# Splitting weight tiles with two DMAs instead of ScalarE and VectorE

## The chip, the cores and the metric

The kernel runs on one core of a Trainium2 chip. The metric is the device time of one execution in microseconds (us). Before the change it is 1057.51 us, the median of three runs (1057.33 to 1058.59). In what follows PE is TensorE, ACT is ScalarE, DVE is VectorE, POOL is GpSimd and SP is SyncE, whose queue issues all DMAs of the kernel before. PEld is TensorE's loading of weights, which runs beside its matmuls.

## The reference

One layer of a decoder trunk on a sequence of 512 tokens and 1024 channels, in float32. After a root-mean-square norm, one matrix `w_in` (1024 x 10 128) projects the tokens into queries, keys and values for three groups of dilated window attention, into the input of a causal pooling branch, into the inputs of a state-space branch (SSD), and into three gates. Each branch ends in its own matrix (`w_a`, `w_b`, `w_c`), the gated sum goes through `w_o` and is added to the input. Then come a second norm, a feed-forward part with a short causal convolution (`ffn_w_up`, 1024 x 5632, and `ffn_w_down`, 2816 x 1024), the second residual and a last norm:

```python
u = rmsnorm(x, ln1_g[i])
proj = u @ w_in[i]
...
merged = gates[:, :, 0] * y_a + gates[:, :, 1] * y_b + gates[:, :, 2] * y_c
x = x + merged @ w_o[i]
x = x + conv_ffn(rmsnorm(x, ln2_g[i]), ffn_w_up[i], ffn_conv_w[i], ffn_conv_b[i], ffn_w_down[i])
return rmsnorm(x, final_g)
```

## The kernel before

**Three products for one.** Every large product is computed in TensorE's type fp32r, which keeps fewer bits than float32. To keep the precision, both operands are split into a high part (the value rounded to fp32r) and a low part (the value less its high part, rounded again), and `mm3` (L215) adds three products in PSUM: high x high, high x low of the activation, and low of the weight x high. The low part of a weight tile is thus first read in the last third of the first block of a job's products.

**Jobs.** All weights are cut into 94 tiles. One tile is a `Job` (L72): its sources in DRAM, its shape and a `body` that issues the products. Most tiles hold 1 MB, as 8 blocks of 128 rows by 256 columns (`jobs_a`, L230: two chunks of 24 matmuls of 512 columns) or as 4 blocks by 512 columns (`jobs_b`, L243: four blocks of tokens, 12 matmuls each). The 8 tiles of `w_o` also hold 1 MB, but each serves two of the four blocks of tokens only, so that its job has 24 matmuls. The tiles of the values are 0.75 or 0.78 MB, the two of `w_a` 0.75 MB, and the last of each half of `w_down` 0.5 MB. The order of the jobs is that of `program` (L1098): pooling input (4 jobs), gate 1 (4), the pooling matrix (1), `w_b` (4); for each attention group values (2) and queries with keys (3), with the SSD inputs (6) after the second group; gate 0 (4), the SSD gate z (4) and gate 2 (4) mixed, `w_a` (2), `w_c` (4), `w_o` (8), `ffn_w_up` (22), `ffn_w_down` (12).

**How a tile comes in.** There are three steps, each with a pool of buffers:

- `fetch` (L168): SP issues the load from DRAM into `raw` (2 buffers).
- `cast` (L177): ACT copies `raw` into `wh` (3 buffers), type fp32r, in two halves.
- `lows` (L197): DVE writes `raw` less `wh` into `wl` (2 buffers), in one instruction.

The main loop (L1273 to L1299) issues, ahead of the products of job n, `prepare` (L1281): the low part of tile n + 1, the cast of tile n + 2 and the load of tile n + 3. With two `raw` buffers the load of tile n + 3 has to wait until the low part of tile n + 1 has been computed. The cast's halves are not issued at once: they are put into the list `second`, and every call of `step` (L143, after each chunk of products) issues one of them; what is left is issued at the start of the next job (L1278). The first four tiles are prepared by hand (L1227 to L1270).

**Order of work.** The instructions of PE, ACT, DVE and POOL run in the order in which the program writes them (`ORDERED`, L1304); each engine is a queue, and an instruction that waits holds up those behind it. `step` also moves along the generators of side work: attention items (`attend`, L489), SSD items (`ssd_item`, L759), norms. POOL's own work is small: the running sums of the pooling branch (`pool_evac`, L621), scalings of the SSD (L787, L802), sums of squares (L865), the attention's weighting (L604), the sum of the branches (L914), half of a norm (L330) and the product of the feed-forward part (L1008). SP's queue holds the weight loads and, among them, the small loads of the side work: `vr` (L468), `al` and `ea` (L766, L772), `wb` (L602).

PSUM has two groups of four banks (`bufs=4`, L101): "mm" for the chunks of the jobs and "sm" for the side work. A chunk's result must be read by ACT or DVE before its bank is used again four chunks later.

Of the kernel before, what the change touches and what calls it, by code (L numbers as in the profile page):

```python
# [10 lines left out]
F32 = mybir.dt.float32  # L11
F32R = mybir.dt.float32r
AF = mybir.ActivationFunctionType
OP = mybir.AluOpType
AX = mybir.AxisListType

P = 128
# [64 lines left out]
def trunk(ctx: ExitStack, tc, out, x, rel_bias, ln1_g, w_in, b_gate, w_a, pool_w, pool_scale, w_b,  # L82
# [3 lines left out]
    act, dve, pool, pe, sp = nc.scalar, nc.vector, nc.gpsimd, nc.tensor, nc.sync  # L86
# [6 lines left out]
    rows = ctx.enter_context(tc.tile_pool(name="rows", bufs=1))  # L93
    wraw = ctx.enter_context(tc.tile_pool(name="wraw", bufs=2))
    whp = ctx.enter_context(tc.tile_pool(name="whp", bufs=3))
    wlp = ctx.enter_context(tc.tile_pool(name="wlp", bufs=2))
    upool = ctx.enter_context(tc.tile_pool(name="upool", bufs=1))
    big = ctx.enter_context(tc.tile_pool(name="big", bufs=NBIG))
    ypool = ctx.enter_context(tc.tile_pool(name="ypool", bufs=2))
# [35 lines left out]
    second = []  # L135

    def flush():
        todo = second[:]
        second.clear()
        for f in todo:  # L140
            f()
# [26 lines left out]
    def fetch(job, cuts=1):  # L168
        raw = job.raw = wraw.tile([P, job.k, job.c], F32, name="raw", tag="raw")
        at = 0  # L170
        for src in job.parts:
            n = src.shape[-1] // cuts
            for i in range(cuts):
                sp.dma_start(raw[:, :, at:at + n], src[:, :, i * n:(i + 1) * n])
                at += n

    def cast(job, cuts=1, spread=False):  # L177

        w = job.c // cuts
        job.high = whp.tile([P, job.k, job.c], F32R, name="wh", tag="wh")  # L180

        def high(i):
            o = slice(i * w, (i + 1) * w)
            act.copy(job.high[:, :, o], job.raw[:, :, o])  # L184

        def at(i):
            high(i)
            if i + 1 < cuts:
                second.append(lambda: at(i + 1))

        if spread:
            second.append(lambda: at(0))
            return
        for i in range(cuts):
            high(i)

    def lows(job, cuts=1, eng=None):  # L197

        w, h = job.c // cuts, job.high
        l = wlp.tile([P, job.k, job.c], F32R, name="wl", tag="wl")  # L200
        job.split = h, l
        for i in range(cuts):
            o = slice(i * w, (i + 1) * w)
            (eng or dve).tensor_tensor(l[:, :, o], job.raw[:, :, o], h[:, :, o].bitcast(F32),  # L204
                                       OP.subtract)
            yield

    def low(job, cuts=1, eng=None):
        for _ in lows(job, cuts, eng):
            pass  # L210
# [926 lines left out]
    weights = [j for j in jobs if isinstance(j, Job)]  # L1137
# [87 lines left out]
    pe.transpose(first[2][:, :KD], g8[:KD, :P], eye[:KD, :KD])  # L1225
    dve.tensor_copy(g1, first[2][:, :KD])
    cast(weights[0], 2)  # L1227
    low(weights[0], 2, pool)
    for k in range(KD):
        turn_scale(1, k % 2 * 4 + k // 2)  # L1230
    for k in range(KD):
        turned(k, 0, bank(k))
    cast(weights[1], 2)
    parts = lows(weights[1], 2)

# [28 lines left out]
    fetch(weights[3])  # L1264
    begin(0, 256, S)
    cast(weights[2])
    low(weights[2])
    begin(1, 256, S)
# [4 lines left out]
    n = 0  # L1273
    for job in jobs:
        if not isinstance(job, Job):
            job.fn()
            continue
        while second:  # L1278
            flush()
        if n >= 2:  # L1280
            def prepare(n=n, later=False):  # L1281

                def rest():
                    if n + 1 < len(weights):
                        low(weights[n + 1])
                    if n + 2 < len(weights):
                        cast(weights[n + 2], 2, spread=not later)
                    if n + 3 < len(weights):
                        fetch(weights[n + 3])
                if later:  # L1290
                    return rest
                rest()

            if job.late:
                job.prepare = prepare
            else:
                prepare()
            job.body(job.split)
        n += 1  # L1299
# [2 lines left out]

# [1 line left out]
ORDERED = {EngineType.PE, EngineType.Activation, EngineType.DVE, EngineType.Pool}  # L1304
NBIG = 54
MIX = "ZZ0zz1ggggaa"
SSD_ORDER = ((0, 0, 1), (1, 0, 1), (0, 1, 1), (2, 0, 1), (1, 1, 1), (3, 0, 1), (2, 1, 1), (3, 1, 1))
WARM = 12
# [29 lines left out]
```

## Time and profile before

| What | Value |
|---|---|
| Median of three runs | 1057.51 us (1057.33 to 1058.59) |
| The profiled execution's own time | 1058.24 us |
| Its span in the trace | 1056.4 us |
| PE busy | 1044.1 us, 99% |
| DVE busy | 576.7 us, 55%; of it 219.2 us in 94 computations of low parts (L204) |
| ACT busy | 430.9 us, 41%; of it 187.2 us in 186 casts of high parts (L184) |
| POOL busy | 134.9 us, 13%, and no DMA is issued from it |
| DMA queue of the loads and stores | 114.68 MB, 35.9% of 16 engines' span |
| Mean TensorE clock granted | 0.998 |

The page has six parts: busy time of each engine; the span in 40 slices; the DMA queues; the chain of work that ended last, followed back through what released each step; the costliest groups of instructions, with busy time, mean length and the idle time of the engine just before them; and the DMA issues. Further views, used below, are the list of waits (who waited for whom), the timeline (instructions in order of time, equal ones merged) and the table of windows (for chosen stretches: busy time of each engine, granted clock, share of the 16 DMA engines in use, GB/s). A matmul's end in the trace is modelled, so "busy" on PE does not mean that it works at its peak; the distance from one matmul's start to the next tells more. The 24 matmuls of one chunk take 5.44 us, so a job of 48 takes 10.9 us and a job of `w_o` about 5.7 us with what lies between.

### The profile page before, as it was taken

To read this page: it belongs to the slowest core of one execution; us is meant where nothing else is said; L and a number is where in the kernel's file an instruction comes from. 1 tells how busy PE (TensorE), PEld (TensorE's weight loads), DVE (VectorE), ACT (ScalarE), POOL (GpSimd) and SP (SyncE) were. 2 spreads that over 40 slices of the span, in tenths; PEclk is the share of its full clock that TensorE was granted. 3 is DMA by queue.
4 is the path that set the end of the run, shared out by engine and by line. 5 is a ranking of instruction groups with operands and counts; after the bars stand their busy time and mean duration, and the time that the engine had idled before them with its cause. 6 is when DMAs were issued, how large, how long until landed. Compare 5 with 4: busy or idle time off the path is not lost.

```text
span 1056.4 us, 13018 instructions
## 1 busy us (share of the span) xinstructions
PE 1044.1 (99%) x5268; PEld 872.5 (83%) x5268; DVE 576.7 (55%) x777; ACT 430.9 (41%) x698; POOL 134.9 (13%) x118
## 2 busy tenths in 40 slices
PE   8999999999999999999999999999999999999997
PEld 8878889898788887787888888898888888888885
DVE  5552523245667538576658756766556565532315
ACT  6343412232545633567555323554444434431311
POOL 1580000000000001100143500002111111110100
PEclk9999999999999999999999999999999999999999
DMA  7236233242221355542252426542322323232312
GB/s 241 77 116 180 80 102 94 86 124 67 83 80 60 81 152 137 150 126 57 69 150 83 157 80 217 184 141 80 117 83 94 105 81 120 80 120 77 103 60 80
DMA packets 116426, 115.50 MB, mean 109 GB/s; under 512 B 5235, under 2 KB 101302, under 8 KB 116367
## 3 DMA queue, kind: packets, MB, share of 16 engines
q1 hardware_dynamic: 116367, 114.68, 35.9%
q8 instruction: 41, 0.67, 0.3%
q14 instruction: 18, 0.15, 0.0%
HBM read 110.87 MB, written 2.22 MB: 107 GB/s over the span
## 4 chain that ended last, share of the span: by engine, by line
PE 91%; DMA 2%; issue 2%; ACT 1%; DVE 1%; SPq 1%; POOL 0%; DVEq 0%; ACTq 0%; POOLq 0%
PE pa L221 35%; PE pu L221 22%; PE pb L221 19%; PE pqk L221 7%; DMA al<-ad 1%; PE ps L512 1%; PE pu L1036 1%; PE ppw L221 1%; PE po L551 1%; PE pt L539 1%; DVE wl L204 1%; DMA raw<-in_w_in_dram 1%; SPq L468 1%; PE py L808 1%; PE pyo L814 1%
## 5 line engine op out<-in xcount | busy, mean ns | idle before, releaser
L204 DVE TENSOR_TENSOR wl<-raw,wh 128x2048 fp32r<-128x2048 f32 (+3 forms) x94 | 219.2, 2333 | 137.9 <-PE pb L221 67.6
L184 ACT CAST wh<-raw 128x1024 fp32r<-128x1024 f32 (+2 forms) x186 | 187.2, 1025 | 104.4 <-PE pb L221 41.0
L221 PE MATMUL pa<-uh,wh 128*128 128x512 f32 x384 | 99.3, 400 | 0.3 <-ACT wh L184 0.3
L1003 DVE SCALAR_TENSOR_TENSOR hc<-pu,fcol,hc 128x510 f32<-128x510 f32 x88 | 65.9, 749 | 54.5 <-ACT hc L1000 52.8
L221 PE MATMUL pa<-ul,wh 128*128 128x512 f32 x384 | 95.0, 389 | 0.0
L221 PE MATMUL pa<-uh,wl 128*128 128x512 f32 x384 | 94.9, 389 | 0.0
L221 PEld LDWEIGHTS pa<-ul,wh 128*128 128x128 f32 x384 | 72.1, 188 | 15.3
L221 PEld LDWEIGHTS pa<-uh,wl 128*128 128x128 f32 x384 | 72.1, 188 | 14.9
L221 PE MATMUL pu<-uh,wh 128*128 128x512 f32 (+1 forms) x352 | 83.7, 380 | 0.0
L221 PEld LDWEIGHTS pa<-uh,wh 128*128 128x128 f32 x384 | 69.9, 188 | 16.5 <-issue 1.7
L221 PE MATMUL pu<-ul,wh 128*128 128x512 f32 (+1 forms) x352 | 83.5, 379 | 0.0
L221 PE MATMUL pu<-uh,wl 128*128 128x512 f32 (+1 forms) x352 | 83.5, 379 | 0.0
L221 PEld LDWEIGHTS pu<-ul,wh 128*128 128x128 f32 x352 | 64.2, 188 | 12.5
L221 PEld LDWEIGHTS pu<-uh,wl 128*128 128x128 f32 x352 | 64.2, 188 | 12.4
L221 PEld LDWEIGHTS pu<-uh,wh 128*128 128x128 f32 x352 | 64.1, 188 | 12.5
L1000 ACT ACTIVATE hc<-pu,fcol,fcol 128x512 f32<-128x512 f32 x40 | 31.2, 780 | 82.1 <-PE pu L221 82.1
L1008 POOL TENSOR_TENSOR hc<-hc 128x512 f32<-128x512 f32 x22 | 31.5, 1433 | 223.3 <-DVE hc L1003 188.2
L787 POOL TENSOR_TENSOR xd<-xc,dec 128x512 f32<-128x512 f32 x6 | 6.4, 1063 | 362.9 <-DVE xc L778 344.3
L533 ACT ACTIVATE sb<-sb,nm 128x128 f32<-128x128 f32 (+1 forms) x72 | 30.1, 419 | 47.0 <-DVE nm L530 33.3
L221 PE MATMUL pb<-wh,fl 128*128 128x512 f32 x176 | 47.7, 389 | 0.0
L221 PE MATMUL pb<-wl,fh 128*128 128x512 f32 x176 | 47.7, 389 | 0.0
L221 PE MATMUL pb<-wh,fh 128*128 128x512 f32 x176 | 47.7, 389 | 0.0
(273 smaller groups left out, 1597.6 us busy)
## 6 DMA issues: line engine op xcount, KB each, us to landing
raw<-in_w_in_dram SPq DMA_DIRECT2D x25, 1024.0 KB
raw<-in_ffn_w_up_dram SPq DMA_DIRECT2D x22, 1024.0 KB
raw<-in_w_in_dram SPq DMA_DIRECT2D x20, 512.0 KB
raw<-in_ffn_w_down_dram SPq DMA_DIRECT2D x10, 1024.0 KB
raw<-in_w_o_dram SPq DMA_DIRECT2D x8, 1024.0 KB
raw<-in_w_in_dram SPq DMA_DIRECT2D x6, 768.0 KB
raw<-in_w_b_dram SPq DMA_DIRECT2D x4, 1024.0 KB
al<-ad SPq DMA_DIRECT2D x16, 256.0 KB
```

The source lines that it names most:

```text
L184: act.copy(job.high[:, :, o], job.raw[:, :, o])
L204: (eng or dve).tensor_tensor(l[:, :, o], job.raw[:, :, o], h[:, :, o].bitcast(F32), OP.subtract)
L221: pe.matmul(ps, l, r, start=first and n == 0, stop=last and n == total - 1)
L468: sp.dma_start(V[g, n][32 * tb:32 * tb + 32, :384], t[n:P:4, :384])
L512: pe.matmul(pss[i][:, o:o + w * P], q[r, n * P:(n + 1) * P], k[r, kb * P:(kb + w) * P], start=True, stop=True)
L533: act.activation(sb[:, off:off + w * P], sb[:, off:off + w * P], AF.Exp, bias=nm[:, n, h:h + 1], accum_out=ls[:, n, h:h + 1])
L539: pe.transpose(pt[:, o:o + P], sb[:, o:o + P], eye)
L551: pe.matmul(po[DH * hh:DH * hh + DH, n * P:(n + 1) * P], V[g, kb + i][:, (2 * c + hh) * DH:(2 * c + hh + 1) * DH], probs[2 * c + hh, nb][: ...
L808: pe.matmul(py[DH * i:DH * i + DH, j * P:(j + 1) * P], xc[:, o:o + DH], als[j // 2][:, lo:lo + P], start=True, stop=True)
L1000: act.activation(t, ps, AF.Identity, bias=ff["c1"][:, ff["b"] + m:ff["b"] + m + 1], scale=fw(2, m))
L1003: dve.scalar_tensor_tensor(t[:, sh:], ps[:, :S - sh], fw(k, m), t[:, sh:], OP.mult, OP.add)
L1008: pool.tensor_tensor(a, a, t, OP.mult)
```

## The change

From tile 4 on, neither ACT's cast nor DVE's subtraction makes the parts of a weight tile. A new function `divide` does. POOL issues a DMA from `raw` to `wh`, both in SBUF, whose destination has the type fp32r, so that the DMA rounds. ACT then writes the negative of `wh` into `wl`, in two halves. After the second half POOL issues a second DMA from `raw` into `wl`, this one with `accum_op=add`: it adds `raw` to what stands in `wl`, which leaves the low part. In `prepare` of job n the tile n + 2 goes through all of `divide`; the first entry of `pieces` does nothing, so that ACT's first half is issued at the second call of `step` in job n, and the second half with the adding DMA at the start of job n + 1. For the feed-forward's first job, whose preparation is late, all is issued at once. The low part of tile 3 is still made by DVE.

The pool of low parts has three buffers instead of two, and the pool `big` of half-row tiles has 50 buffers instead of 54.

```diff
-    wlp = ctx.enter_context(tc.tile_pool(name="wlp", bufs=2))
+    wlp = ctx.enter_context(tc.tile_pool(name="wlp", bufs=3))
...
+    def divide(job, spread=False):
+        w = job.c // 2
+        h = whp.tile([P, job.k, job.c], F32R, name="wh", tag="wh")
+        l = wlp.tile([P, job.k, job.c], F32R, name="wl", tag="wl")
+        job.split = h, l
+        o = [slice(i * w, (i + 1) * w) for i in range(2)]
+
+        def minus(i):
+            act.mul(l[:, :, o[i]], h[:, :, o[i]].bitcast(F32), -1.0)
+            if i:
+                pool.dma_start(l, job.raw, accum_op=OP.add)
+
+        pieces = [lambda: None, lambda: minus(0), lambda: minus(1)]
+
+        def at(i):
+            pieces[i]()
+            if i < 2:
+                second.append(lambda: at(i + 1))
+
+        pool.dma_start(h, job.raw)
+        if spread:
+            second.append(lambda: at(0))
+        else:
+            for f in pieces:
+                f()
...
-                    if n + 1 < len(weights):
-                        low(weights[n + 1])
+                    if n == 2:
+                        low(weights[3])
                     if n + 2 < len(weights):
-                        cast(weights[n + 2], 2, spread=not later)
+                        divide(weights[n + 2], spread=not later)
                     if n + 3 < len(weights):
                         fetch(weights[n + 3])
...
-NBIG = 54
+NBIG = 50
```

## The prediction

> **What bounds the kernel now.** I read the page's busy times first, then the chain and the DMA queue, then PE's waits, and last the windows and the timeline around one weight tile. The page:
>
> ```profile
> span 1056.4 us, 13018 instructions
> PE 1044.1 (99%) x5268; PEld 872.5 (83%) x5268; DVE 576.7 (55%) x777; ACT 430.9 (41%) x698; POOL 134.9 (13%) x118
> ...
> q1 hardware_dynamic: 116367, 114.68, 35.9%
> ...
> PE 91%; DMA 2%; issue 2%; ACT 1%; DVE 1%; SPq 1%; POOL 0%; DVEq 0%; ACTq 0%; POOLq 0%
> ...
> L204 DVE TENSOR_TENSOR wl<-raw,wh 128x2048 fp32r<-128x2048 f32 (+3 forms) x94 | 219.2, 2333 | 137.9 <-PE pb L221 67.6
> L184 ACT CAST wh<-raw 128x1024 fp32r<-128x1024 f32 (+2 forms) x186 | 187.2, 1025 | 104.4 <-PE pb L221 41.0
> ```
>
> PE carries the chain. DVE and ACT, whose work is replaced, stand beside it with a half of the span free. The list of PE's waits from 45 to 1040 us (PE idle, releaser) has two entries:
>
> ```profile
> PE pcb L782 <- DVE ea L816: 1.0, 1, 1.0
> PE pbt L753 <- ACT o L557: 0.4, 1, 0.4
> ```
>
> So 1.4 us is about all that a faster preparation can give back; the rest of PE's idle time lies before 45 us and in the last 7 us, where no tile is divided by the new path. What matters is whether the new path delivers a tile as often as PE uses one: 10.9 us for a job of 48 matmuls, 5.7 us in `w_o` (8 jobs between 640.7 and 686.5 us).
>
> Windows around one 1 MB load (columns: stretch, then busy time and count on PE, PEld, DVE, ACT, POOL, granted clock, DMA share, GB/s), and SP's timeline:
>
> ```profile
> 730.00:731.00 1.00, 1.00 (x6) 0.84 (x5) 0.77 (x2) 0.00 (x0) 0.05 (x1) 1.00 0.55 63
> 732.00:733.00 1.00, 1.00 (x6) 0.83 (x5) 0.00 (x0) 0.00 (x0) 0.23 (x1) 1.00 1.07 368
> 734.00:735.00 1.00, 1.00 (x6) 0.81 (x6) 0.61 (x1) 1.00 (x2) 0.00 (x0) 1.00 0.09 18
> ...
> 649.00:651.00 2.00, 2.00 (x11) 1.65 (x10) 0.72 (x2) 0.72 (x2) 1.29 (x1) 1.00 1.05 406
> ```
>
> ```profile
> 729.39 0.37 SPq L174 DMA_DIRECT2D raw<-in_ffn_w_up_dram  x1
> ```
>
> The load is issued at 729.39 and its bytes stop at about 734.3: **F = 4.9 us**. At the 406 GB/s of the best window, 1 MB takes 2.6 us of the 16 engines; the other 2.3 us is latency, in which the engines could serve something else.
>
> **The change part by part.**
>
> *DVE loses 90 subtractions, ACT's casts become multiplications.* 94 stand in the row, 4 remain (two halves of tile 1, tiles 2 and 3): 219.2 − 2 x 1.22 − 2 x 2.29 = 212 us less on DVE. Of it only the 1.4 us above can reach PE. The 180 halves on ACT keep their number and shape (128x1024, 1.04 us each from the row): 0. They come half a job later; the work behind them on ACT is the evacuations of PSUM, and the cover is the four banks of "mm", some 22 us of PE. Once ACT waits longer than that for a rounding DMA, the wait reaches PE; the loop below contains it.
>
> *180 DMAs on POOL, 2 x 91.3 MB.* Before, no DMA starts on POOL and no DMA adds or rounds, so this is bounded from both sides. A 1 MB copy inside SBUF: at least 1.3 us of the engines (twice the best window, as nothing is read from DRAM), at most 5.2 (half of it). I take 2.6, the load's own price, and 2.3 of latency: **C = 4.9**. The adding DMA: from 2.6, if it costs as much as a copy, to 10.4, four times that. It has to read two operands for each value that it writes, so I take two copies' time: 5.2 + 2.3, **A = 7.5**. The two halves on ACT between the DMAs: 2 x 1.04 = **M = 2.1**.
>
> The Trainium skill, "Collectives: The Full Stack", section "The bandwidth ceiling: the fold count and why AG ≠ RS ≠ AR", states that a DMA that adds runs at half the rate of a copy because of its two source reads, measured there as 62.28 against 32.35 GB/s. By that rule the engines' time per tile is 10.4 us; were the add as cheap as a copy, it would be 7.8. No run here shows it yet.
>
> *The new wait: `raw` is held through the add.* The load of tile n + 3 waits until the adding DMA of tile n + 1 has read `raw`; before, it waited for DVE's 2.3 us. One buffer thus goes through F, C, M, A in series: 4.9 + 4.9 + 2.1 + 7.5 = 19.4 us, of which 10.4 are DMA engine time and 9.0 are not. With two buffers circulating, a transfer meets the other tile's for 10.4/19.4 = 54% of its time and is stretched by that: 10.4 x 1.54 = 16.0, plus 9.0 = 25.0 us for two tiles, **12.5 us a tile**. (Bounds: 10.4 if the engines never rest, (20.8 + 9.0)/2 = 14.9 if every transfer meets another in full.) By the same working a 0.75 MB tile takes 10.2 and a 0.5 MB tile about 8 us.
>
> Against PE's pace, stage by stage: gate 1, pooling matrix and `w_b`, 9 tiles x 1.6 = 14; first values and `qk` 2 x 1.4 + 3 x 1.6 = 8; second group to SSD inputs, jobs of 14 to 15.5 us, about 0; third values and `qk`, 57.9 against 50 us = 8; 411 to 581 us, 12 jobs of 14 us, 0; `w_a` 2 x 2.1 = 4; `w_c` 4 x 1.6 = 6; **`w_o` 8 x 6.8 = 54**; `ffn_w_up` 22 x 1.5 = 33; `ffn_w_down` 10 x 1.6 + 2 x 2.5 = 21. Sum 148. The third low buffer lets preparation run about one tile ahead after the slow stage that ends at 581: −12.
>
> *POOL's order.* The first adding DMAs stand behind the running sums of the pooling branch, which end on POOL at 62.4 (chunk 5) and 77.0 us (chunk 7). Job 4 starts at 60.7 and reads its low part at 64.3; the add is issued at about 63.4 and lands at 71: 7 us. The next lands at about 87, against 77.1 + 7: 3 more. Together +10. Later on, what stands behind a waiting DMA on POOL is L787, L865, L604, L914, L330 and L1008; for these POOL is 87% free, and their readers (SSD states, sums, the feed-forward's `later`) come a step or more behind: 0.
>
> *SP's order.* The load now waits up to 7 us longer, and `vr`, `al`, `ea` and `wb` are issued behind it. PE is not idle there and the SSD's DMAs are asked for one to four steps ahead: I take 0, at most 8 items x 7 = 56. *Buffers:* a low tile's 8 KB per partition come from four buffers of `big`; `ffn_w_up`'s end uses most of them; 0, at most one evacuation (about 2 us) in each of its last few jobs.
>
> Sum: 148 − 12 + 10 = +146. The profiled execution took 1058.24 us (its span 1056.4 and 1.8 around it), 0.7 above the median of the runs. 1057.5 + 146 gives about **1204 us**.
>
> **The rivals.**
>
> *The add costs no more than a copy.* Engine time 7.8, alone 16.8, in pairs 7.8 x 1.46 + 9.0 = 20.4, so 10.2 us a tile: jobs of 48 are fed. Left are `w_o` 8 x 4.5 = 36, `w_a` and the half tiles 4, POOL's order 6, less 12: +34, **1092 us**. For it: every row here shows one rate, near 400 GB/s. Against: two reads per write.
>
> *The DMAs' arithmetic is slower than their copying.* Rounding and adding at half the load's rate each: engine time 2.6 + 5.2 + 5.2 = 13.0, 14.8 us a tile, and now the DMA engines are the bound in nearly all stages. Deficits as above: 35 + 18 + 6 + 18 + 7 + 8 + 16 + 73 + 84 + 44 = 309, with the other two terms **about 1365 us**; if the add were four copies, 17.2 us a tile, about 1580. For it: nothing in the trace shows arithmetic in a DMA, fast or slow.
>
> *Not slower: the preparation stays hidden.* It decides in `w_o`: the pair must circulate in 2 x 5.7 = 11.4 us, plus some 3 us for the tile in hand. With copies inside SBUF at 1.3 us and no latency to speak of, the loop is 4.9 + 1.3 + 2.1 + 1.3 = 9.6 us alone, and it holds. Then the 1.4 us of PE's waits is the only price: **1056 us**. For it: the load's latency may be DRAM's. Against: each adding DMA has to end before ACT, SP or PE goes on.
>
> **How the numbers follow.** Forecast (two reads) 38%, add at a copy's price 31%, slow arithmetic 22%, hidden 9%. 0.2%, here 2.1 us, is about what a measurement can tell from no change; hidden gives 4% faster by more than that (if the modelled ends of matmuls cover more waits than the 1.4 us shown) and 5% within it, the other three 91% slower. The range 1070 to 1450 leaves out the hidden case (9%), the part of the slow case with an add at three or four copies' price (8%), and a little of the cheap one (3%).
>
> **What would show it.** Right: DVE's L204 row falls to 4 instructions; POOL issues 180 DMAs and a new queue carries some 180 MB; PE gains idle time released by DMAs into `wl` (or by ACT behind a DMA into `wh`), most per job in `w_o`; loads follow each other in pairs about 25 us apart in `ffn_w_up`; a first stall near 64 us. Wrong: if the pairs come every 21.8 us and only `w_o` loses, the add costs a copy; if the DMA share stays near 1 through the feed-forward with under 3 x 1 MB per 12.5 us, the arithmetic is slow; if the idle time of PE is released by SSD tiles near 370 to 520 us, SP's order, which I set to 0, is the cause.

## The result and the profile after

The changed kernel takes **1293.4 us** (median of four runs, 1291.5 to 1297.0) against 1057.4 us for the kernel before (four runs beside them): 1.2235 times as long, 95% interval 1.2205 to 1.2265. The profiled execution has a span of 1289.7 us. The forecast was 1204 us; its direction and its largest stages came, and 89 us more.

The page of the changed kernel. (Its lines are shifted: the products of `mm3` are L249, before L221; ScalarE's negative is L207, the adding DMA L209, the rounding DMA L218.)

```profile
span 1289.7 us, 13415 instructions
PE 1118.3 (87%) x5268; PEld 906.7 (70%) x5268; DVE 366.5 (28%) x687; ACT 431.0 (33%) x698; POOL 248.3 (19%) x298
...
q0 software_dynamic: 25920, 182.59, 55.7%
q1 hardware_dynamic: 116367, 114.68, 28.6%
...
DMA 47%; issue 27%; PE 11%; ACT 7%; POOL 5%; SPq 1%; DVE 1%; POOLq 0%; ACTq 0%; DVEq 0%
...
L207 ACT ACTIVATE wl<-wh 128x1024 fp32r<-128x1024 f32 (+2 forms) x180 | 179.6, 1024 | 614.7 <-DMA wh<-raw 515.4
L209 POOL DMA_DIRECT2D wl<-raw x90 | 79.4, 883 | 871.2 <-ACT wl L207 796.8
...
wh<-raw POOLq DMA_DIRECT2D x80, 1024.0 KB, 8.8
wl<-raw POOLq DMA_DIRECT2D x80, 1024.0 KB, 7.0
```

DVE has lost 210 us, and nobody gains by it. A second queue, `q0`, carries the 182.6 MB of the two new DMAs; with the loads' `q1` it keeps the 16 DMA engines busy for 84% of the span, against 36% before. PE carries 11% of the chain instead of 91%. ACT's 180 negatives last as long as the casts before, but wait 515 us for rounding DMAs; POOL's adding DMAs wait 797 us for ACT.

PE's list of waits (line, whom it waited for: us in all, times, longest) held 1.4 us behind the start. Now it begins:

```profile
PE pb L249 <- DMA wl<-raw: 66.4, 23, 9.5
PE pa L249 <- DMA wl<-raw: 34.4, 18, 6.8
PE pu L249 <- DMA wl<-raw: 23.7, 16, 2.0
PE pqk L249 <- DMA wl<-raw: 12.0, 6, 5.2
```

Each is a product waiting for an adding DMA. The first such stall, 3.9 us, comes at 64 us, as forecast. I set the starts of the same matmuls side by side in the two traces, stage by stage; the difference is the time lost in a stage. (The forecast counted the opening of the feed-forward within `ffn_w_up`.)

| Stage (us in the kernel before) | Forecast | Lost |
|---|---|---|
| pooling, gate 1, pooling matrix, `w_b` (38.8 to 160.6) | 24 | 21.0 |
| first values and first `qk` (to 210.9) | 8 | 8.5 |
| second values, `qk`, SSD inputs (to 366.1) | 0 | 12.4 |
| third values, `qk` (to 411.3) | 8 | 17.2 |
| gate 0, z (to 533) | 0 | 13.2 |
| z and gate 2 (to 581) | 0 | 24.2 |
| `w_a`, `w_c` (to 640.7) | 10 | 8.2 |
| `w_o` (to 690.3) | 54 | 57.1 |
| opening of the feed-forward and `ffn_w_up` (to 929.4) | 33 | 44.3 |
| `ffn_w_down` | 21 | 28.0 |
| lead of the third low buffer | −12 | 0 |
| sum | 146 | 234 |

Two stages in windows (stretch, then busy time and count on PE, PEld, DVE, ACT, POOL, granted clock, DMA share, GB/s): `w_o` and `ffn_w_up`, first in the kernel before, then after.

```profile
640.74:690.28 49.54, 49.54 (x244) 41.70 (x243) 35.71 (x52) 25.82 (x43) 5.18 (x4) 1.00 0.56 186
699.96:929.44 229.48, 229.48 (x1059) 192.06 (x1058) 135.63 (x129) 97.72 (x129) 29.93 (x21) 1.00 0.30 98
```

```profile
744.89:851.47 106.58, 67.46 (x243) 52.50 (x242) 18.61 (x43) 25.96 (x41) 16.46 (x20) 0.79 0.92 260
874.29:1135.02 260.73, 237.00 (x1058) 192.98 (x1058) 80.28 (x108) 96.38 (x128) 56.43 (x63) 0.99 0.88 243
```

The DMA share rises from 0.56 to 0.92 and from 0.30 to 0.88: the engines that carry the transfers are nearly full in both stages.

### The profile page after: what moved, and what is told of

Its sections match the earlier page's. It is cut to its first block, busy times and chain, and to the rows that moved or that the text cites. A ratio compares the mean times of both kernels' runs of the same rounds, so it can differ in the third digit from the quotient of the medians.

```text
span 1289.7 us, 13415 instructions
## 1 busy us (share of the span) xinstructions
PE 1118.3 (87%) x5268; PEld 906.7 (70%) x5268; DVE 366.5 (28%) x687; ACT 431.0 (33%) x698; POOL 248.3 (19%) x298
## 4 chain that ended last, share of the span: by engine, by line
DMA 47%; issue 27%; PE 11%; ACT 7%; POOL 5%; SPq 1%; DVE 1%; POOLq 0%; ACTq 0%; DVEq 0%
DMA wh<-raw 21%; DMA wl<-raw 15%; ACT wl L207 6%; DMA raw<-in_w_in_dram 4%; PE pa L249 4%; DMA raw<-in_ffn_w_up_dram 3%; PE pb L249 3%; PE pqk L249 2%; POOL wl L209 1%; DMA raw<-in_ffn_w_down_dram 1%; POOL wh L218 1%; PE pu L249 1%; DMA wb<-wd 1%; POOL psw L657 1%; DMA raw<-in_w_c_dram 1%
## 5 line engine op out<-in xcount | busy, mean ns | idle before, releaser
L207 ACT ACTIVATE wl<-wh 128x1024 fp32r<-128x1024 f32 (+2 forms) x180 | 179.6, 1024 | 614.7 <-DMA wh<-raw 515.4
L209 POOL DMA_DIRECT2D wl<-raw x90 | 79.4, 883 | 871.2 <-ACT wl L207 796.8
L249 PE MATMUL pa<-uh,wl 128*128 128x512 f32 x384 | 102.2, 411 | 25.0 <-DMA wl<-raw 24.9
L249 PE MATMUL pu<-uh,wl 128*128 128x512 f32 (+1 forms) x352 | 86.6, 389 | 23.7 <-DMA wl<-raw 23.7
L249 PEld LDWEIGHTS pa<-uh,wl 128*128 128x128 f32 x384 | 74.7, 197 | 45.6 <-issue 25.1
L249 PE MATMUL pa<-uh,wh 128*128 128x512 f32 x384 | 103.6, 413 | 0.3 <-ACT wh L184 0.3
L249 PE MATMUL pa<-ul,wh 128*128 128x512 f32 x384 | 95.0, 389 | 0.0
L249 PEld LDWEIGHTS pu<-uh,wl 128*128 128x128 f32 x352 | 63.5, 190 | 41.9 <-issue 30.0
L249 PE MATMUL pu<-uh,wh 128*128 128x512 f32 (+1 forms) x352 | 85.6, 386 | 2.1 <-ACT uh L350 2.1
L249 PEld LDWEIGHTS pa<-uh,wh 128*128 128x128 f32 x384 | 73.1, 197 | 19.2 <-issue 3.2
L249 PE MATMUL pu<-ul,wh 128*128 128x512 f32 (+1 forms) x352 | 83.5, 379 | 0.0
L249 PEld LDWEIGHTS pa<-ul,wh 128*128 128x128 f32 x384 | 72.1, 188 | 15.3
L249 PEld LDWEIGHTS pu<-uh,wh 128*128 128x128 f32 x352 | 65.8, 193 | 15.7 <-ACT uh L350 2.4
L249 PEld LDWEIGHTS pu<-ul,wh 128*128 128x128 f32 x352 | 64.2, 188 | 12.5
L218 POOL DMA_DIRECT2D wh<-raw x90 | 58.7, 652 | 48.2 <-issue 9.3
L249 PE MATMUL pb<-wl,fh 128*128 128x512 f32 x176 | 50.9, 409 | 18.6 <-DMA wl<-raw 18.6
L249 PE MATMUL pb<-wl,mgh 128*128 128x512 f32 x64 | 24.7, 521 | 39.1 <-DMA wl<-raw 39.1
L249 PEld LDWEIGHTS pb<-wl,fh 128*128 128x128 f32 x176 | 33.9, 197 | 28.9 <-issue 22.2
L249 PE MATMUL pb<-wh,fh 128*128 128x512 f32 x176 | 50.4, 406 | 0.0
L249 PE MATMUL pb<-wh,fl 128*128 128x512 f32 x176 | 49.8, 403 | 0.0
L249 PE MATMUL pqk<-uh,wl 128*128 128x512 f32 x144 | 39.1, 417 | 12.0 <-DMA wl<-raw 12.0
```

Source lines behind the costliest of these rows:

```text
L207: act.mul(l[:, :, o[i]], h[:, :, o[i]].bitcast(F32), -1.0)
L209: pool.dma_start(l, job.raw, accum_op=OP.add)
L218: pool.dma_start(h, job.raw)
L249: pe.matmul(ps, l, r, start=first and n == 0, stop=last and n == total - 1)
```

## The experiments

### What each DMA costs: copy for add, rounding alone, adding alone

The second DMA without `accum_op`, so that nothing is added. It still rounds, since its destination has the type fp32r:

```diff
-                pool.dma_start(l, job.raw, accum_op=OP.add)
+                pool.dma_start(l, job.raw)
```

> The adding DMA becomes a plain rounding copy of the same tile into the same buffer, with the same issue and the same waits; what is left out is the addition, so the low parts are wrong. If the add costs two reads and the loop over the two raw buffers sets the pace, the second DMA lands in about 4.5 us instead of 7.0, the engines' time per tile falls from 10.3 to 7.7 us, a tile of the feed-forward's first matrix takes 10.9 us (PE's pace) instead of 12.8, and the whole takes 1120 to 1160 us. If the add costs no more than a copy, nothing changes: about 1293 us.

Measured: 1122.7 us, ratio 1.0619 (1.0604 to 1.0635).

The rounding DMA alone, with the low part by DVE as before:

```diff
     def divide(job, spread=False):
-        ...
+        job.high = whp.tile([P, job.k, job.c], F32R, name="wh", tag="wh")
+        pool.dma_start(job.high, job.raw)
...
-                    if n == 2:
-                        low(weights[3])
+                    if n + 1 < len(weights):
+                        low(weights[n + 1])
```

> High parts by the rounding DMA, low parts by VectorE as in the kernel before. The raw buffer is held through load, one DMA and VectorE's 2.3 us: about 14 us for one buffer, 7 us a tile, below PE's 10.9 and above the 5.7 us of a w_o job. Loop theory: 1065 to 1090 us, the loss in w_o. If the rounding DMA with its issue on GpSimd were the main cause: above 1150 us.

Measured: 1080.4 us, 1.0221 (1.0205 to 1.0236). This kernel has the change's buffer counts too. Of its loss 11.1 us lie in `w_o` and 13.3 in gate 0 and z, where the buffer counts alone lose 11.8 (the last experiment below).

The adding DMA alone, ACT making high part and negative:

```diff
         def minus(i):
+            act.copy(h[:, :, o[i]], job.raw[:, :, o[i]])
             act.mul(l[:, :, o[i]], h[:, :, o[i]].bitcast(F32), -1.0)
...
-        pool.dma_start(h, job.raw)
```

> High parts by ScalarE's cast as before, low parts by ScalarE's negative and the adding DMA. One buffer is held through load (5 to 6), cast and negative (4.2) and the add (6.5 to 7): about 17 us, 8.5 a tile. Loop theory: 1085 to 1140 us, most of it in w_o, none in the feed-forward. If the adding DMA by itself were the cause: about 1200 us or more, with stalls in the feed-forward.

Measured: 1167.0 us, 1.105 (1.1031 to 1.1068), over the 1140 that I expected at most. `w_o` loses 42.2 us, and the feed-forward, for which I expected nothing, 14.8.

The pages' list of DMA issues (KB each, median us from issue to landing), of the kernel with a rounding copy for the add:

```profile
wh<-raw POOLq DMA_DIRECT2D x80, 1024.0 KB, 6.3
wl<-raw POOLq DMA_DIRECT2D x80, 1024.0 KB, 4.3
```

and of the two others, rounding alone and adding alone:

```profile
wh<-raw POOLq DMA_DIRECT2D x80, 1024.0 KB, 4.7
```

```profile
wl<-raw POOLq DMA_DIRECT2D x80, 1024.0 KB, 7.7
```

A DMA that rounds lands after 4.7 us (forecast C = 4.9), the one in the add's place, which rounds too, after 4.3, one that adds after 7.0 to 7.7 (forecast A = 7.5). In the changed kernel's trace an 8 KB packet of the add takes 628 ns or a little more and one of the rounding 325 ns or a little more, where no packet of a load runs beside it (medians 644 and 328); 128 of them on 16 engines are 5.0 and 2.6 us. A load of 1024 packets at 46 ns is 2.9. The addition alone is worth 1293 − 1123 = 171 us of the 236. That it costs twice a copy is shown; whether by its second read or by its arithmetic, no run here separates. The Trainium skill, "Collectives: The Full Stack", section "The bandwidth ceiling: the fold count and why AG ≠ RS ≠ AR", states half rate for the adding DMAs of a collective and gives the two source reads as the reason; 628 against 325 ns agrees with the rate.

The two halves of the change cost 24 us (some 12 of them by the buffer counts) and 110 us alone, and 236 together: they don't add up; they share engines, a queue and the buffers. Adding alone cost more than expected. Its chain in `w_o` (start, length, piece) shows what holds it:

```profile
723.73 7.01 DMA wl<-raw
...
730.80 9.00 DMA raw<-in_w_o_dram
...
739.87 4.58 issue
```

Add, then the load into the buffer that the add gives free, then ACT's four pieces, then the next add: 20.6 us for two tiles, the loop over two `raw` buffers of the forecast, without the rounding step.

### The order on POOL and on SP

Two candidates for the stages that the forecast set to 0 are other work on POOL and SP. First, the attention's weighting from POOL to DVE:

```diff
-                pool.tensor_tensor(OT[g, c], OT[g, c], wb, OP.mult)
+                dve.tensor_tensor(OT[g, c], OT[g, c], wb, OP.mult)
```

> The attention's nine weighting products move from GpSimd to VectorE, so the adding DMA of that stage no longer stands behind products that wait for wb. If GpSimd's order causes the 24 us that the stage from z to gate 2 loses against the kernel before, 8 to 20 of them come back there: 1273 to 1285 us. If SP's order causes them (the weight load behind the wb loads), nothing: 1290 to 1296 us.

Measured: 1299.2 us, 1.2299 of before; z and gate 2 lose 28.3 us, not less. Second, the load of `wb` from SP's queue to ACT's:

```diff
-                    sp.dma_start(wb[DH * hh:DH * hh + DH, :],
+                    act.dma_start(wb[DH * hh:DH * hh + DH, :],
```

> The 18 wb loads of the attention's weighting are issued from ScalarE's queue instead of SP's, so that weight loads and wb loads no longer stand behind each other. If SP's order causes the loss from z to gate 2, 8 to 20 of the 24 us come back: 1273 to 1285 us. If GpSimd's order does: within 4 us of 1293.

Measured: 1297.2 us, 1.2281; z and gate 2 lose 25.6 us. Neither is the cause there.

### The order on ACT

The timeline of ACT in the changed kernel, in the stage of z and gate 2 (start, length, instruction, in brackets idle time before it and its releaser):

```profile
649.23 1.06 ACT L207 ACTIVATE wl<-wh 128x1024 fp32r<-128x1024 f32 x1 [9.14 <-DMA wh<-raw]
650.19 1.12 ACT L917 CAST yth<-xs 128x512 fp32r<-128x512 f32 x2
651.33 1.28 ACT L320 ACT_TABLE_LOAD   x1
652.63 0.20 ACT L320 ACTIVATE sq<-v 128x4 f32<-128x4 f32 x1
655.98 0.62 ACT L640 CAST ah<-o 128x512 fp32r<-128x512 f32 x1 [3.14 <-DVE o L638]
656.50 1.05 ACT L207 ACTIVATE wl<-wh 128x1024 fp32r<-128x1024 f32 x1
```

The first half of the negative holds ACT for 9 us until the rounding has landed. The side work that was held up then stands ahead of the second half, so that this adding DMA is issued 6 us later than the data allows. It is one of the longer distances: over the 12 tiles from gate 0 to gate 2 the halves stand 3 us apart in the mean. So I issued both halves at once, which also brings the second half and the add forward from the start of the next job:

```diff
-        pieces = [lambda: None, lambda: minus(0), lambda: minus(1)]
+        pieces = [lambda: None, lambda: (minus(0), minus(1)), lambda: None]
```

> Both halves of ScalarE's negative are issued one behind the other at the second place, and the adding DMA right behind them; nothing else differs from the changed kernel. Theory (the order on ScalarE costs the 17 us of the third group and the 24 us of the mixed gates, which the prediction set to 8 and 0: the second half stands behind a job's side work, and the add comes 6 us late): these two stages lose at most 10 us each, the feed-forward's first matrix stays at 12.8 us a tile because the halves already stand together there, and the whole takes 1255 to 1275 us. Rival (these stages are late because the DMAs themselves are late, or because ScalarE's first half holds up the side work while it waits for the rounding DMA, which it still does here): the two stages stay within 4 us of 17 and 24, and the whole takes 1285 to 1300 us.

Measured: 1251.6 us, 1.1858 (1.1826 to 1.189), 42 us less than the changed kernel. The same place now:

```profile
617.57 1.99 ACT L207 ACTIVATE wl<-wh 128x1024 fp32r<-128x1024 f32 x2
```

The third group loses 7.4 us instead of 17.2, gate 0 and z 1.5 instead of 13.2, the second values to SSD inputs 7.8 instead of 12.4, z and gate 2 14.0 instead of 24.2; `w_o` still 57.1 and `ffn_w_up` 29.1. The order on ACT is shown as the cause of 36 us in these four stages. z and gate 2 stay above the 10 us that I expected; what their other 14 us are was not settled.

### The loop over two buffers

Three kernels shorten the time for which `raw` is held. The first lets the rounding DMA read DRAM itself, in two pieces, so that `raw` serves the add alone:

```diff
-        pool.dma_start(h, job.raw)
+        c0 = 0
+        for src in job.parts:
+            n = src.shape[-1]
+            for i in range(0, job.k, 4):
+                pool.dma_start(h[:, i:min(i + 4, job.k), c0:c0 + n], src[:, i:min(i + 4, job.k), :])
+            c0 += n
```

> The rounding DMA reads the weight from DRAM instead of from raw (two DMAs of half a tile each), and everything else stays. The DMA engines have as much to do per tile as in the changed kernel (10.3 us or a little more), but raw is held through load, negative and add alone: about 17 instead of 25.7 us. If the loop over two raw buffers sets the pace: 1150 to 1200 us, the feed-forward back at 11 us a tile. If the throughput of the DMA engines sets it: 1285 to 1320 us.

Measured: 1681.8 us, 1.591. It separated nothing, because a new wait came in, as POOL's list of waits says:

```profile
POOL wh L222 <- issue: 588.2, 81, 9.1
```

The second pieces stood 7.3 us each on POOL, for nothing that the profile shows as a release. The same with twice the memory for the descriptors of POOL's DMAs:

```diff
-NBIG = 50
+NBIG = 49
...
-    nc = _bacc.Bacc("TRN2", target_bir_lowering=False, num_devices=1, dynamic_dma_scratch_size=1024)
+    nc = _bacc.Bacc("TRN2", target_bir_lowering=False, num_devices=1, dynamic_dma_scratch_size=2048)
```

> The rounding DMA reads from DRAM, as in the run before, where the second half's DMA waited 8.35 us on GpSimd before it was issued. Here the ring of descriptors is twice as large (dynamic_dma_scratch_size 2048 instead of 1024; NBIG is 49). If that wait was the full ring, the idle time ahead of these DMAs on GpSimd falls from 588 us to under 100, and the loop (raw held through load, negative and add alone) can be read: loop theory 1150 to 1250 us, feed-forward near 11 us a tile; throughput theory 1285 to 1350. If the wait was not the ring: still about 1680.

Measured: 1420.8 us (1419.6 to 1421.9), 1.3451; that wait fell to 60.1 us in 9 times, so it came from there. But the two queues now take 65.8% and 26.3% of the engines, 92% together: a rounding DMA that reads rows of 1 KB from DRAM costs more engine time than one that reads 8 KB rows in SBUF (61 ns for each KB, 3.9 us a tile, against 2.6), and the loop can't be told from the engines. Both DMAs from DRAM, without `raw`, on top of the last edit:

```diff
-                pool.dma_start(l, job.raw, accum_op=OP.add)
+                c0 = 0
+                for src in job.parts:
+                    n = src.shape[-1]
+                    for q in range(0, job.k, 2):
+                        pool.dma_start(l[:, q:min(q + 2, job.k), c0:c0 + n], src[:, q:min(q + 2, job.k), :], accum_op=OP.add)
+                    c0 += n
...
-                    if n + 3 < len(weights):
-                        fetch(weights[n + 3])
```

> From tile 4 on raw and its load are gone: the rounding DMA and the adding DMA both read DRAM, in two and four pieces, with the larger ring. Nothing circulates through raw any more, so loop theory gives a pace set by the transfers in a row for three low buffers: 1060 to 1130 us. If SWDGE pieces of 1 KB are slow by themselves, as the 61 ns against 46 ns a packet in the run with the high part from DRAM suggest, or if their issue on GpSimd is, above 1200 us.

Measured: 1586.3 us, 1.5017, far off, and no test of the loop: POOL now carries 26% of the chain, as the adding DMAs, cut in four pieces, took 1.5 us each of it:

```profile
L213 POOL DMA_DIRECT2D wl<-in_w_in_dram x176 | 215.5, 1515 | 273.4 <-ACT wl L207 226.0
```

So the direct way, a third `raw` buffer:

```diff
-    wraw = ctx.enter_context(tc.tile_pool(name="wraw", bufs=2))
+    wraw = ctx.enter_context(tc.tile_pool(name="wraw", bufs=3))
...
-            s = SG[b, lo + m] = T("sg")
+            s = SG[b, lo + m] = SG[1, m - 4] if b == 1 and m >= 4 else T("sg")
...
-NBIG = 50
+NBIG = 46
```

> Three buffers for the tiles as loaded instead of two. Room for it comes from the half-row tiles: 46 instead of 50, with chunks 4 to 7 of gate 1 written over chunks 0 to 3, so that their values are left out (every instruction stays). Theory (the loop load, round, negate, add over two buffers is what limits the feed-forward's first matrix): with three buffers the same loop gives a tile every 8.6 us or what the DMA engines allow (about 10.1 us: 2.6 for the load, 2.5 for the rounding, 5.0 for the add), so that the first feed-forward matrix is fed at PE's 10.9 us and loses under 8 us instead of 31, the output matrix loses 30 to 42 instead of 57, the second feed-forward matrix under 14 instead of 28, and the whole takes 1170 to 1215 us. Rival (the software queue or the DMA engines limit by throughput at 12.8 us a tile): the first feed-forward matrix still loses 27 to 35 us, and the whole takes 1270 to 1300 us.

Measured: 1292.9 us, 1.2239 (1.2218 to 1.2259): nothing gained. `ffn_w_up` loses 32.6 us, `w_o` 57.3. This kernel also has four half-row tiles fewer than the changed one, but no stage loses more than 1.4 us more than there, so they show no cost of their own. My theory, and with it the forecast's account of the 12.5 us, is not what alone limits here. In the changed kernel the loop over the buffers can be followed link by link; its chain in `ffn_w_up`:

```profile
928.30 6.99 DMA wl<-raw
...
935.34 7.58 DMA raw<-in_ffn_w_up_dram
...
943.54 7.98 DMA wh<-raw
...
951.54 2.02 ACT wl L207 x2
```

With three buffers another loop of the same length takes its place. POOL's timeline with three buffers (the next add follows at 952.03):

```profile
926.52 0.87 POOL L209 DMA_DIRECT2D wl<-raw  x1 [11.00 <-ACT wl L207]
927.11 0.85 POOL L218 DMA_DIRECT2D wh<-raw  x1
...
939.53 0.89 POOL L209 DMA_DIRECT2D wl<-raw  x1 [6.96 <-ACT wl L207]
940.12 0.85 POOL L218 DMA_DIRECT2D wh<-raw  x1
```

ACT's, for the tile rounded by the DMA of 940.12:

```profile
949.59 2.01 ACT L207 ACTIVATE wl<-wh 128x1024 fp32r<-128x1024 f32 x2 [4.06 <-DMA wh<-raw]
```

The rounding of tile n + 2 is issued right behind the add of tile n + 1 and goes through the same queue after it: 0.6 us to its issue, 9.4 to its landing, 2.0 for the negative, 0.4 to the next add. That is 12.5 us a tile, and no number of `raw` buffers changes it.

### The rounding ahead of the add

This order can be turned round, with three `raw` buffers and two low ones (each tile's negative is then made a job later):

```diff
+    def rounded(job):
+        job.high = whp.tile([P, job.k, job.c], F32R, name="wh", tag="wh")
+        pool.dma_start(job.high, job.raw)
+
+    def rest_of(job):
+        ...
+        for i in range(2):
+            o = slice(i * w, (i + 1) * w)
+            act.mul(l[:, :, o], h[:, :, o].bitcast(F32), -1.0)
+        pool.dma_start(l, job.raw, accum_op=OP.add)
...
-                        divide(weights[n + 2], spread=not later)
+                        rounded(weights[n + 2])
+                    if n > 2 and n + 1 < len(weights):
+                        rest_of(weights[n + 1])
```

> The rounding DMA of tile n + 2 is issued on POOL ahead of the adding DMA of tile n + 1 instead of behind it, and both halves of the negative of tile n + 1 stand at the start of job n, a whole job after that tile was rounded; for this the tiles as loaded have three buffers and the low parts two. Nothing is left out. Theory (with three buffers for the loaded tiles the first feed-forward matrix still took 12.7 us a tile because of the order in the one software queue: add 7.0, the next rounding behind it 9.4 after its issue, negative 2.0, next add): the chain from add to rounding to add is cut, the tiles follow at PE's 10.9 us or the DMA engines' 10.1, and the first feed-forward matrix loses at most 12 us instead of 31; ScalarE never waits for a rounding DMA, so the third group and the mixed gates lose under 8 us each; the output matrix still loses 35 to 45 (8 tiles of about 10.3 us against 5.7); the whole takes 1120 to 1190 us. Rival (the DMA engines or the software queue can't pass more than a tile in 12.5 us, in whatever order): the first feed-forward matrix loses 27 to 35 us, the output matrix 52 or more, and the whole takes over 1220 us.

Measured: 1247.5 us, 1.1805 (1.1779 to 1.183): 46 us better than the changed kernel, and over 1220. It splits the question. `w_o` loses 44.6 us instead of 57.1, z and gate 2 11.1 instead of 24.2: in `w_o`, where neither halves together nor three buffers had gained anything, the order in the queue counted; in the gates most of it may be ACT's order again, which had given 10 us there. The third group still loses 17.6 us: its chain goes through the SSD's load of `al` on SP's queue, 7.9 us, behind which ACT's negative stands. `ffn_w_up` loses 38.4, even more than the rival's 27 to 35. (The kernel with `wb` on ACT's queue, in which nothing of the feed-forward was changed, lost 38.3 there, so 38 may be no worse than the changed kernel's 31.) The windows of this kernel for `w_o` and `ffn_w_up`, columns as above:

```profile
718.47:812.64 94.17, 61.62 (x244) 48.47 (x242) 20.54 (x49) 26.08 (x42) 15.29 (x18) 0.82 0.98 285
831.72:1099.64 267.92, 241.37 (x1060) 196.34 (x1058) 77.95 (x106) 98.62 (x129) 60.05 (x63) 0.97 0.90 245
```

In `w_o` the DMA engines are full, at 98%, 94.2 us for 8 tiles. In `ffn_w_up` neither order nor buffers changed the pace. Between adds there (mean of 15 to 18 intervals) and the DMA share of the stage, for the four kernels:

| Kernel | us between adds | DMA share | engine time per tile |
|---|---|---|---|
| changed | 12.8 | 0.88 | 11.3 |
| halves together | 12.5 | 0.89 | 11.1 |
| three `raw` buffers | 12.9 | 0.87 | 11.2 |
| rounding first | 12.5 | 0.90 | 11.3 |

The last column is the product of the two before it. A tile keeps all 16 engines busy for 11.1 to 11.3 us, and PE needs 10.9 us for its job: even without a gap the stage would be late, but by 0.2 to 0.4 us a tile, some 4 to 8 us over the stage. The rest of its loss lies in the gaps. (The engine time is a sum over packets, and packets take longer where transfers meet; undisturbed it would be 10.5 us.) What leaves the gaps in the last kernel can be seen on POOL and in its chain:

```profile
897.10 0.58 POOL L199 DMA_DIRECT2D wh<-raw  x1
897.67 0.95 POOL L208 DMA_DIRECT2D wl<-raw  x1
911.93 0.55 POOL L199 DMA_DIRECT2D wh<-raw  x1 [13.31 <-DMA raw<-in_ffn_w_up_dram]
912.59 0.88 POOL L208 DMA_DIRECT2D wl<-raw  x1
```

```profile
897.50 13.81 DMA raw<-in_ffn_w_up_dram
```

A load that took 4.9 us alone takes 13.8 beside a rounding and an add; the rounding waits for it, and the next add stands behind the rounding on POOL. Packets that started in stretches of this trace (load: 1 KB on SP's queue; rounding and add: 8 KB on POOL's):

```
us from start   load   rounding and add
898 to 902        97   128
902 to 905       841     6
905 to 912        90   122
```

The load's first packet starts at 899.6. From there to 901.5 it starts 62 packets beside 61 of the rounding, then alone 280 in each microsecond, and its last 90 stretch over 6 us, to 911.0, beside the add. The Trainium skill, "DMA: Bandwidth & Descriptors", section "SWDGE vs HWDGE vs iDMA", says that a DMA engine goes round-robin between the queues that feed it; 62 packets of 1 KB against 61 of 8 KB agree with turns of one packet, whatever its size, so that small packets lose. The load's end doesn't test this: from 907.5 to 909.5 at most one of its packets starts in half a microsecond, beside 12 to 16 of the add, and on how many engines any were left isn't known.

### The buffers alone

The kernel before, with the change's buffer counts alone:

```diff
-    wlp = ctx.enter_context(tc.tile_pool(name="wlp", bufs=2))
+    wlp = ctx.enter_context(tc.tile_pool(name="wlp", bufs=3))
...
-NBIG = 54
+NBIG = 50
```

> The kernel before with only the change's buffer counts: three low tiles and 50 half-row tiles. The prediction set the smaller pool to 0 and counted the third low buffer as a gain only where preparation is slow, which it isn't here: 1056 to 1059 us. If the four missing half-row tiles hold up evacuations, up to 2 us in each of the last jobs of the first feed-forward matrix: 1060 to 1070 us.

Measured: 1069.0 us, 1.0124 (1.0107 to 1.014). PE's waits behind the start now begin with the SSD:

```profile
PE pxs L776 <- DVE ea L816: 4.1, 2, 2.3
PE pcb L782 <- DVE ea L816: 1.9, 1, 1.9
PE ps L512 <- DVE ea L816: 1.5, 1, 1.5
```

All of the loss lies between 411 and 533 us (8.6 and 3.2 us in gate 0 and z); `ffn_w_up`, which the prediction named, loses nothing. With 50 instead of 54 half-row tiles the SSD's work gets its tiles too late: SP's loads of `al`, which fill such tiles, now wait 14 us for PE and DVE to be done with a tile (before, in the same stages, 4.5 us at the longest):

```profile
SPq L766 <- PE pyo L814: 14.2, 1, 14.2
SPq L766 <- DVE sb L526: 14.0, 1, 14.0
```

The two counts were not tried one by one. That the same shortage makes part of the changed kernel's 13.2 us there is not shown; with ACT's halves together only 1.5 us are left.

## Why the prediction was right, and where it was wrong

**What bounds the kernel, and the direction: right.** PE was full, DVE's 212 us could give back 1.4, and the new path had to deliver a tile as fast as PE used one. It didn't.

**The prices C, M and A: right within 0.5 us.** C 4.7 (4.9), M 2.0 (2.1), A 7.0 to 7.7 (7.5). F, 4.9 alone, grew beside the others, to 7.6 in the chain of `ffn_w_up`. Engine time per tile was 11.1 to 11.3 instead of 10.4 us (5.0 + 2.6 + 2.9 = 10.5 undisturbed; the rest comes where transfers meet). The rival with the add at a copy's price is excluded by the copy in its place (1123 us), that of slow arithmetic by a rounding that costs the engines no more than a load (2.6 against 2.9 us), and the hidden one by the result.

**12.5 us a tile: the number right, its reason incomplete.** Intervals between adds in `ffn_w_up` average 12.8 us. But the step "one buffer goes through F, C, M, A in series" isn't the only thing that gives this number: with three buffers it stayed. The chain add, rounding, negative, add through one software queue is as long, and behind both stand DMA engines whose 11.2 us a tile exceed PE's 10.9 by a little. The prediction had 10.4 there and so took the loop for the only limit. That `w_o` (57 for 54) and `ffn_w_up` itself (31 for 33) came out right is in part luck: two loops happen to have one length, and the engines are nearly full.

**The zeros: wrong.** The three stages put at 0 lost 49.8 us, over half of the 88 us between the table's sums. For ACT's halves the prediction had "0. They come half a job later", and this was the failed step: its cover, the four banks, was set against an evacuation held up, not against the adding DMA behind the second half. From the second values to gate 2 the negative's two halves stood 2.4 us apart in the mean and up to 8.0. Issuing them later and apart cost 36 us in four stages put at 0 or 8. The 0 for POOL's order held for the weighting, and the 0 for SP's order for `wb`; for the SSD's loads on SP it wasn't tested by itself.

**The lead of the third low buffer, −12: wrong.** No stage shows it: a lead has to be built by a path that is faster than PE, and where it was to be built the path was already late.

**The opening of the feed-forward: mis-sized.** It has 9.7 us of work, and the prediction gave it a job's 1.5 us; it lost 13.1. PE waits there for adding DMAs (5.7 us) and rounding ones (1.2). The loss stays with ACT's halves together (12.9) and shrinks with a copy for the add (9.2). That `w_o` leaves its tiles late doesn't explain it alone: with the add alone `w_o` lost 42.2 us and the opening 2.9. The rest of its cause stays open.

**`ffn_w_down`, 28 for 21:** its tiles, too, come at the pace of the transfers (DMA share 0.88 while they come); the term's 1.6 us a tile was too small by about 0.6.

**Big buffers, 0: wrong in the kernel before** (+12 us), at another place than the one I looked at.

**POOL's order at the start, +10:** with the stages around it 21 us came for 24.

## What to carry to other kernels

Before work is moved from a half-idle engine to DMAs, add up the DMA engines' time per tile (a DMA that adds in SBUF cost two copies here) and set it against the bounding engine's time for that tile. Here it was 11.2 us against 10.9, and neither a third buffer nor another order hid it. Several loops can have the same length, so a number that comes out right is no proof of the loop it was derived from; lengthen or cut each one by itself. And when an instruction that issues a DMA is split in two among other work, the distance between the parts can delay every transfer behind it.

## What I had not expected of the hardware

- A load in 1 KB packets is slowed far more than in proportion by 8 KB packets of POOL's queue: 62 packets in 1.9 us instead of 280 in one, and 13.8 us in all instead of 4.9.
- Two DMAs of 512 KB with rows of 1 KB on POOL's queue held POOL for 7.3 us per tile (588.2 us in 81 waits) until the descriptors' memory was doubled.
- The granted clock is lower where PE idles much: 0.79 in `w_o`, where PE is busy for 63% of the time and the same matmuls take 67.5 instead of 49.5 us, and 0.99 in `ffn_w_up`, where it is busy for 91%. Some of a stall shows up as slower matmuls, not as a wait: PE's busy time rose from 1044 to 1118 us with no product added.
